# Rounding the next weight block behind the evacuation and the side work, in the stages with transposed results

## The chip, the cores and the metric

The kernel runs on one core of a Trainium2 chip. The metric is the device time of one execution in microseconds; the time before is 1458.11 us, the median of three runs (1457.9 to 1459.06).

## What is computed

Two transformer blocks run on 256 tokens of width 1024, all in float32. The first has an HGRN2 mixer (a gated linear recurrence), a causal multi-scale pooling branch and an MLP with squared ReLU. The second has block attention with a gMLP branch, cross attention over 256 memory rows, and a PEER layer: each token picks 16 of 16384 experts in each of 8 heads by product keys. The core of it is a long row of matrix products, cut to what matters:

```python
proj = x @ w_in                                   # 7 parts of 1024 columns
merged = sigmoid(gate_a) * a + sigmoid(gate_b) * b
x = layer_norm(ALPHA * x + merged @ w_out)
x = layer_norm(ALPHA * x + square(relu(x @ w_up)) @ w_down)
...
y_a = moba_attention(q, k, v) @ moba_w_proj
y_b = gmlp_spatial_gating(gu, gv) @ gmlp_w_proj
x = x + (sigmoid(gate_a) * y_a + sigmoid(gate_b) * y_b) @ w_out
x = x + memory_cross_attention(rmsnorm(x), mem)
x = x + peer_ffn(rmsnorm(x))                      # top-k over product keys
```

The kernel computes the PEER layer over all experts: gelu of the tokens times all down rows, multiplied by a sparse route, times all up rows.

## The kernel before

**Weights.** All weights come as blocks of 128 x 1024 float32 (512 KB), in the fixed order of `plan`: 478 of them. `load` (L122) issues the DMA of one block on SP's queue into a raw buffer (7 of them in the first part of the program, 4 afterwards). `feed` (L138) rounds the block to its high half with one ScalarE copy (L156). `low` (L163) takes the rest, raw minus high, with one VectorE subtraction (L170). TensorE multiplies three times for each 128 x 128 tile: high weights by high input, high by low, low by high (L213 to L215).

**Who decides the order.** The program runs under a manual schedule: TensorE, VectorE and ScalarE execute in the order in which the program writes their instructions. `fill` (L173) feeds blocks until `cap` of them are out (4 in most stages, 5 to 12 around some) and calls `ahead` (L134), which issues the loads for which there is room. `release` (L193) gives a used block back. A new block's rounding has to wait until TensorE has read the block whose buffer it takes.

**Two kinds of stages.** `gemm_n` (L232) gives results with tokens on the partitions, and is not touched. `gemm_t` (L201) gives transposed results, output features on the partitions and 256 tokens as columns. Its outputs come in pairs of 128 features, which share one PSUM bank of `ps_p`; there are two such banks, so a pair can only start when the pair before the last has been evacuated. Where the inner depth is 8 tiles, one weight block is one output of 128 features, and a pair takes two blocks. Where it is 4 (the two projections L1067 and L1077), a block is a whole pair.

**The end of a block** in `gemm_t` (L217 to L225), in this order: release the block, `fill`, evacuate the pair if it is complete (`evac`), then `pump`, `low` and `behind`. `pump` (L93) advances the side work: generators (`hgrn_all` L696, `attend` L915, `gating` L1014, `mem_side` L1049, `routing` L1203, `route` L1334) and closures put off with `later`. `behind` (L321) writes the low halves of results that an evacuation has put off (`split_late` L317).

**Evacuations** that the text speaks of: `evac_sig` (L731, ScalarE tanh, then VectorE); `evac_gate` (L1029: VectorE multiplies by `rall` into `xr` L985, ScalarE tanh L333, VectorE L334); `evac_yb` (L1039, VectorE only, L1040); `evac_a` (L782) and `evac_ya` (L1071): two VectorE operations (L784/785, L1073/1074), then ScalarE rounds the sum (L318), and VectorE takes the low half in `behind` (L323). In the expert stages (`down`, L1321) it is one ScalarE gelu (L1323).

**Side work** that the text speaks of: in `attend` each of four units goes through `scores` (TensorE, VectorE mask L935, ScalarE copies L938), `softmax` (VectorE maximum L900, L901, four ScalarE exponentials L904), a division L909, `turn` (TensorE transposes, ScalarE copies L948) and `output` (ScalarE L329, VectorE L330). `mem_side` runs four ScalarE squares over the memory (L450) and scales it (L1057) by a root that VectorE works out in between. `key_scores` (L1281) copies router scores with ScalarE (L1287) for `routing` on VectorE.

Of the kernel before, what the change touches and what calls it, by code (L numbers as in the profile page):

```python
# [30 lines left out]
def kernel(ctx: ExitStack, tc: tile.TileContext, A: dict, out: bass.AP):  # L31
# [34 lines left out]
    def bp(name, shape=(P, 2, T)):  # L66
        return bank(ps_p, name, shape)
# [4 lines left out]
    def f32(ap):  # L72
        return ap.bitcast(F32)
# [19 lines left out]
    def pump():  # L93
        for s in list(sides):
            s[2] += s[1]
            while s[2] >= 1.0:
                s[2] -= 1.0
                if next(s[0], None) is None:
                    sides.remove(s)
                    break  # L100
        for d in list(deferred):
            d[0] -= 1
            if d[0] <= 0:
                deferred.remove(d)
                d[1]()
# [13 lines left out]
    def room():  # L119
        return 7 if raw_x else 4  # L120
# [13 lines left out]
    def ahead():  # L134
        while plan and plan[0] is not None and len(loaded) + len(half) < room():
            load()

    def feed(beside=None):  # L138

        if not loaded:  # L140
            load()
        raw, kind, cs = loaded.pop(0)
        parts = len(cs)
        wst["out"] += 1
        own, lent = wst["own"] < 4 and kind != 1, 0
        if own:
            wst["own"] += 1
            pc = spl.tile([P, 2, 1024], F32R, tag="w", name="w")
        elif extra:
            pc, lent = extra.pop(0), 1  # L150
        else:
            pc = b8("wb", (P, 2, 1024), F32R)
        for i, x in enumerate(cs):
            if beside:
                beside(i)
            S.activation(pc[:, 0, x], raw[:, x], AF.Copy)  # L156
            if parts > 1:
                V.tensor_tensor(pc[:, 1, x], raw[:, x], f32(pc[:, 0, x]), OP.subtract)
        ready.append((pc[:, 0, :], pc[:, 1, :], own, lent, pc))
        if parts == 1:  # L160
            half.append((pc, raw))

    def low(n=None):  # L163

        if n is None:
            if wst["hold"] or not wst["calm"] and (pend[0] or pend[1]):
                return
            n = 2
        for pc, raw in half[:n]:
            V.tensor_tensor(pc[:, 1, :], raw, f32(pc[:, 0, :]), OP.subtract)  # L170
        del half[:n]

    def fill():  # L173
        while wst["out"] < wst["cap"] and (loaded or plan and plan[0] is not None):
            if (loaded[0][1] if loaded else plan[0][2]) == 2 and wst["own"] >= 4:
                break
            if not loaded and len(half) >= room():
                break
            feed()
        ahead()  # L180

    def take():
        if not ready:
            feed()
        pc = ready.pop(0)
        for i, x in enumerate(half):
            if x[0] is pc[4]:
                low(i + 2)
                break
        low()  # L190
        return pc

    def release(pc):  # L193
        wst["out"] -= 1
        wst["own"] -= pc[2]
        wst["cap"] -= pc[3]
# [4 lines left out]
    def gemm_t(nblk, nk, xs, evac):  # L201

        xh, xl = xs
        pc, f = None, 1024
        for b0 in range(0, nblk, 2):
            ps = bp("pt")
            for j in range(2):
                b, o = b0 + j, ps[:, j, :]
                for k in range(nk):
                    if f == 1024:  # L210
                        pc, f = take(), 0
                    hi, lo = pc[:2]
                    PE.matmul(o, hi[:, f:f + P], xh(b, k, ALL), start=(k == 0), stop=False)  # L213
                    PE.matmul(o, hi[:, f:f + P], xl(b, k, ALL), start=False, stop=False)  # L214
                    PE.matmul(o, lo[:, f:f + P], xh(b, k, ALL), start=False, stop=(k == nk - 1))  # L215
                    f += P
                if f == 1024:  # L217
                    release(pc)
                    fill()
                if j:  # L220
                    evac(b0, 2, ps, ALL)
                if f == 1024:
                    pump()
                    low()
                    behind()  # L225
        behind()
# [94 lines left out]
    def behind():  # L321
        for hi, lo, src in late_lo:
            V.tensor_tensor(lo, src, f32(hi), OP.subtract)  # L323
        late_lo.clear()
# [218 lines left out]
    def proj_fq(u):  # L543
        h0 = u * 4
        fT, kT = h4("fk")
        qT, gc = h4("qg")
        hst[u] = (fT, kT, qT, gc)

        def evac_f(b, n, ps, ts):
            sg = t2("sg", (P, 2, T))  # L550
            S.activation(sg, ps, AF.Tanh, scale=0.5)
            for j in range(2):
                h = h0 + b + j
                V.tensor_scalar(fT[:, b + j, :], sg[:, j, :], oml[:, h:h + 1], lb[:, h:h + 1], op0=OP.mult, op1=OP.add)
            V.tensor_scalar(kT[:, b:b + 2, :], fT[:, b:b + 2, :], -1.0, 1.0, op0=OP.mult, op1=OP.add)

        def evac_q(b, n, ps, ts):
            sg = t2("sg", (P, 2, T))
            S.activation(sg, ps, AF.Tanh, scale=0.5)
            V.scalar_tensor_tensor(qT[:, b:b + 2, :], sg, 1.0, ps, op0=OP.add, op1=OP.mult)  # L560

        gemm_t(4, 8, xk_of(xs), evac_f)
        gemm_t(4, 8, xk_of(xs), evac_q)
# [167 lines left out]
    def evac_sig(dst):  # L731
        def f(b, n, ps, ts):
            sigmoid(dst[:, b:b + n, ts], ps)
        return f

    gemm_t(8, 8, xk_of(xs), evac_sig(sgo))
    gemm_n([evac_v], 8, 1024, xt_of(xs))
    os_, pls = [], []
# [871 lines left out]
```

## Time and profile before

| what | value |
|---|---|
| median of three runs | 1458.11 us |
| the profiled execution's own time | 1457.66 us |
| its span, first to last instruction | 1456.0 us |
| mean granted TensorE clock | 0.998 |
| VectorE busy | 1075.9 us (74%) |
| ScalarE busy | 717.5 us (49%) |
| weight blocks | 478 of 512 KB |

The page gives for each engine the time in which at least one of its instructions ran. TensorE's ends are modelled, so its busy share is not its share at peak. The waits view names, for each idle gap, the instruction that ended it. The windows view counts instructions in a stretch: a matmul over 256 columns comes every 0.112 us at full clock.

### The profile page before, as it was taken

What the parts mean: (1) busy time and instruction counts of PE and PEld (TensorE: products, weight loads), DVE (VectorE), ACT (ScalarE), POOL (GpSimd) and SP (SyncE); (2) the same over time, 40 slices, a digit from 0 to 9 for tenths busy, and PEclk for the clock granted to TensorE, in tenths of its full rate; (3) what the DMA queues carried; (4) which work ended last, traced back from release to release, by engine and by line L of the source; (5) the groups of instructions that cost most, each with busy time, mean ns of one, the idle gap of its engine ahead of it and who ended that gap; (6) DMA issues with size and microseconds to landing.
All of it is one profiled execution on the core that took longest, in us unless ns stands there. A gap on an engine that the chain in (4) does not pass through costs nothing.

```text
span 1456.0 us, 25899 instructions
## 1 busy us (share of the span) xinstructions
PE 1432.4 (98%) x10420; PEld 1304.6 (90%) x10420; DVE 1075.9 (74%) x1895; ACT 717.5 (49%) x933; POOL 33.2 (2%) x68
## 2 busy tenths in 40 slices
PE   8999999999998999999999999999999999999997
PEld 8989998998877899879999999999899787888885
DVE  6867788665498678756999957888645999855555
ACT  5663464554363566644554544444444444444443
POOL 1004000000001000000000000000000000000000
PEclk9999999999999999999999999999999999999999
DMA  8554465566656456515456555455555555555662
GB/s 289 175 160 145 146 222 203 198 215 192 196 181 216 129 191 202 177 55 191 158 174 218 193 190 182 161 174 174 174 189 189 168 180 200 174 190 189 200 191 86
DMA packets 72762, 263.42 MB, mean 181 GB/s; under 512 B 8240, under 2 KB 8752, under 8 KB 72128
## 3 DMA queue, kind: packets, MB, share of 16 engines
q1 hardware_dynamic: 70416, 252.48, 53.7%
q0 software_dynamic: 1936, 8.98, 1.8%
q8 instruction: 82, 1.34, 0.4%
q14 instruction: 40, 0.33, 0.1%
q10 hardware_dynamic: 288, 0.30, 0.1%
HBM read 259.62 MB, written 2.10 MB: 180 GB/s over the span
## 4 chain that ended last, share of the span: by engine, by line
PE 90%; DVE 8%; ACT 1%; issue 1%; DMA 0%; SPq 0%; DVEq 0%; ACTq 0%
PE py L1404 24%; PE pn L247 16%; PE pt L213 15%; PE pt L215 14%; PE pt L214 14%; PE gt L1360 2%; DVE w L170 2%; DVE slots L1194 1%; DVE wb L170 1%; DVE slots L1192 1%; PE hs L637 1%; DVE slots L1197 1%; PE tr L466 0%; PE tr L345 0%; ACT w L156 0%
## 5 line engine op out<-in xcount | busy, mean ns | idle before, releaser
L156 ACT ACTIVATE w<-raw 128x1024 fp32r<-128x1024 f32 (+1 forms) x415 | 435.8, 1051 | 540.1 <-PE pt L215 250.9
L170 DVE TENSOR_TENSOR w<-raw,w 128x1024 fp32r<-128x1024 f32 x409 | 497.8, 1221 | 157.4 <-ACT w L156 156.2
L213 PE MATMUL pt<-h4h,w 128*128 128x256 f32 x1088 | 305.5, 281 | 0.0
L215 PE MATMUL pt<-h4h,w 128*128 128x256 f32 x1088 | 302.4, 278 | 0.1
L214 PE MATMUL pt<-h4l,w 128*128 128x256 f32 x1088 | 302.0, 278 | 0.0
L1404 PE MATMUL py<-w,wh 128*128 128x512 f32 (+1 forms) x1024 | 283.2, 391 | 0.4 <-ACT wh L329 0.4
L1404 PEld LDWEIGHTS py<-w,wh 128*128 128x128 f32 x1024 | 189.4, 188 | 38.9 <-ACT wh L329 0.8
L215 PEld LDWEIGHTS pt<-h4h,w 128*128 128x128 f32 x1088 | 204.9, 188 | 0.8 <-DVE w L170 0.7
L213 PEld LDWEIGHTS pt<-h4h,w 128*128 128x128 f32 x1088 | 204.8, 188 | 0.1
L214 PEld LDWEIGHTS pt<-h4l,w 128*128 128x128 f32 x1088 | 204.6, 188 | 0.1
L1404 PE MATMUL py<-w,wl 128*128 128x512 f32 x512 | 159.4, 390 | 0.2 <-DVE wl L330 0.2
L213 PE MATMUL pt<-xh,w 128*128 128x256 f32 x384 | 110.7, 288 | 5.2 <-ACT w L156 5.2
L1404 PEld LDWEIGHTS py<-w,wl 128*128 128x128 f32 x512 | 96.1, 188 | 20.8 <-DVE wl L330 0.5
L214 PE MATMUL pt<-xl,w 128*128 128x256 f32 x384 | 109.2, 284 | 0.0
L215 PE MATMUL pt<-xh,w 128*128 128x256 f32 x384 | 109.1, 284 | 0.0
L330 DVE TENSOR_TENSOR wl<-slots,wh 128x512 fp32r<-128x512 f32 (+1 forms) x68 | 44.3, 657 | 77.1 <-ACT wh L329 77.1
L213 PEld LDWEIGHTS pt<-xh,w 128*128 128x128 f32 x384 | 74.3, 194 | 5.8 <-ACT w L156 5.5
L170 DVE TENSOR_TENSOR wb<-raw,wb 128x1024 fp32r<-128x1024 f32 x63 | 74.8, 1219 | 5.4 <-ACT wb L156 5.3
L214 PEld LDWEIGHTS pt<-xl,w 128*128 128x128 f32 x384 | 74.0, 193 | 0.4
L215 PEld LDWEIGHTS pt<-xh,w 128*128 128x128 f32 x384 | 73.7, 192 | 0.3
L156 ACT ACTIVATE wb<-raw 128x1024 fp32r<-128x1024 f32 x63 | 63.5, 1048 | 16.0 <-issue 7.4
L1354 DVE TENSOR_TENSOR oo<-oo,rt 128x512 f16<-128x512 f16 x128 | 48.7, 421 | 2.2
(487 smaller groups left out, 2391.0 us busy)
## 6 DMA issues: line engine op xcount, KB each, us to landing
raw<-in_peer_down_dram SPq DMA_DIRECT2D x128, 512.0 KB, 3.5
raw<-in_peer_up_dram SPq DMA_DIRECT2D x128, 512.0 KB, 3.6
raw<-in_w_up_dram SPq DMA_DIRECT2D x32, 512.0 KB, 4.7
raw<-in_w_down_dram SPq DMA_DIRECT2D x32, 512.0 KB, 3.9
raw<-in_w_gb_dram SPq DMA_DIRECT2D x16, 512.0 KB, 3.9
raw<-in_w_ga_dram SPq DMA_DIRECT2D x16, 512.0 KB, 4.6
raw<-in_w_out_dram SPq DMA_DIRECT2D x16, 512.0 KB, 4.0
raw<-in_peer_q_dram SPq DMA_DIRECT2D x16, 512.0 KB, 4.6
```

Source lines behind the costliest of these rows:

```text
L156: S.activation(pc[:, 0, x], raw[:, x], AF.Copy)
L170: V.tensor_tensor(pc[:, 1, :], raw, f32(pc[:, 0, :]), OP.subtract)
L213: PE.matmul(o, hi[:, f:f + P], xh(b, k, ALL), start=(k == 0), stop=False)
L214: PE.matmul(o, hi[:, f:f + P], xl(b, k, ALL), start=False, stop=False)
L215: PE.matmul(o, lo[:, f:f + P], xh(b, k, ALL), start=False, stop=(k == nk - 1))
L247: PE.matmul(o, xx(k, t), ww[:, kk * n + h * 512:kk * n + h * 512 + 512], start=(k == 0 and i == 0), stop=(k == nk - 1 and i == 2))
L330: V.tensor_tensor(lo, src, f32(hi), OP.subtract)
L637: PE.matmul(ps[:, h, :], kk[:, h, tok(t)], qq[:, h, tok(t)], start=True, stop=True)
L1192: V.max(vals[:, c], src)
L1354: V.tensor_tensor(o2[:, i].rearrange("p t (a two) -> p t a two", two=2), q2, turn(1 + i, t0, n), OP.mult)
L1360: PE.matmul(ps[:, u, :], p1[:, u, :], p2[:, i, u, :], start=(i == 1), stop=(i == 2))
L1404: PE.matmul(o, x[:, i % 2, tok(t)], w[:, c], start=(apart[1] == 0 if apart else first and i == 0) and n == 0, stop=(last and i == 7 and n ...
```

## The change

In `gemm_t`, the call of `fill` moves from right behind `release` to behind the evacuation and behind `pump`; `low` and `behind` still follow it. Nothing is added or removed: the same roundings, loads, evacuations and side steps are issued, and the operations of TensorE and VectorE keep their order. On ScalarE the rounding of the next block changes places with the evacuation's and the side work's operations of the same block end; on SP's queue there are only weight loads there, and their order stays.

```diff
@@ -216,11 +216,11 @@
                     f += P
                 if f == 1024:
                     release(pc)
-                    fill()
                 if j:
                     evac(b0, 2, ps, ALL)
                 if f == 1024:
                     pump()
+                    fill()
                     low()
                     behind()
         behind()
```

## Rows read from the trace of the kernel before

**Rows 1.** The page, part 1: busy time and share of the span, by engine.
```profile
PE 1432.4 (98%) x10420; PEld 1304.6 (90%) x10420; DVE 1075.9 (74%) x1895; ACT 717.5 (49%) x933; POOL 33.2 (2%) x68
```

**Rows 2.** Waits of TensorE: total us, times, longest.
```profile
PE rr L980 <- DVE rs_y L426: 3.4, 1, 3.4
...
PE pt L213 <- DVE mg L1073: 0.6, 1, 0.6
...
PE ho L668 <- ACT sx L652: 0.5, 1, 0.5
```

**Rows 3.** Waits of all engines: total us, times, longest.
```profile
DVE w L170 <- ACT w L156: 156.2, 129, 9.3
```

**Rows 4.** Windows: TensorE, weight loads, VectorE, ScalarE, GpSimd busy; clock, DMA, GB/s.
```profile
0.00:20.00 20.00, 14.77 (x85) 13.91 (x86) 11.99 (x30) 12.29 (x19) 4.75 (x27) 1.00 0.90 326
...
300.00:320.00 20.00, 20.00 (x179) 20.00 (x178) 13.58 (x15) 11.71 (x15) 1.05 (x2) 1.00 0.65 192
...
440.00:460.00 20.00, 16.20 (x78) 12.98 (x77) 19.30 (x44) 7.37 (x10) 3.98 (x5) 1.00 0.81 277
...
520.00:540.00 20.00, 20.00 (x177) 19.70 (x177) 14.35 (x21) 12.56 (x23) 0.00 (x0) 1.00 0.50 158
```

**Rows 5.** VectorE's groups from 492 to 574 us: busy, mean ns, idle before.
```profile
L170 DVE TENSOR_TENSOR w<-raw,w 128x1024 fp32r<-128x1024 f32 x20 | 24.4, 1219 | 0.2 <-ACT w L156 0.2
...
L985 DVE TENSOR_TENSOR xr<-pt,rall 128x512 f32<-128x512 f32 x8 | 5.5, 685 | 0.7 <-PE pt L215 0.7
```

**Rows 6.** ScalarE's groups from 492 to 574 us.
```profile
L156 ACT ACTIVATE w<-raw 128x1024 fp32r<-128x1024 f32 x20 | 21.1, 1056 | 11.4 <-PE pt L215 5.6 <-issue 5.5
...
L904 ACT ACTIVATE e<-e,mx 128x256 f32<-128x256 f32 x8 | 4.0, 498 | 3.4 <-DVE mx L901 3.4
...
L1057 ACT ACTIVATE nrm<-mem,rs_y 128x512 f32<-128x512 f32 x4 | 2.7, 716 | 2.6 <-DVE rs_y L426 2.6
L318 ACT ACTIVATE m2h<-mg 128x512 fp32r<-128x512 f32 x4 | 2.5, 630 | 5.6 <-DVE mg L1074 5.6
...
L450 ACT ACTIVATE jk<-mem 128x512 f32<-128x512 f32 x4 | 2.5, 621 | 0.0
```

**Rows 7.** Timeline of ScalarE around a softmax step: start us, us, operation.
```profile
512.12 1.06 ACT L156 ACTIVATE w<-raw 128x1024 fp32r<-128x1024 f32 x1 [0.41 <-PE pt L215]
514.74 0.51 ACT L904 ACTIVATE e<-e,mx 128x256 f32<-128x256 f32 x1 [1.55 <-DVE mx L901]
...
516.72 1.04 ACT L156 ACTIVATE w<-raw 128x1024 fp32r<-128x1024 f32 x1
```

**Rows 8.** Timeline of VectorE in the same stretch.
```profile
514.47 0.17 DVE L901 TENSOR_SCALAR mx<-mx 128x4 f32<-128x4 f32 x1
514.55 1.22 DVE L170 TENSOR_TENSOR w<-raw,w 128x1024 fp32r<-128x1024 f32 x1
515.69 0.68 DVE L985 TENSOR_TENSOR xr<-pt,rall 128x512 f32<-128x512 f32 x1
```

**Rows 9.** Timeline of VectorE in the projection with `evac_ya`.
```profile
564.54 0.69 DVE L1073 TENSOR_TENSOR mg<-pt,sga 128x512 f32<-128x512 f32 x1
...
567.61 0.68 DVE L1073 TENSOR_TENSOR mg<-pt,sga 128x512 f32<-128x512 f32 x1
```

**Rows 10.** Timeline of VectorE at the end of the stage with `evac_a`.
```profile
225.26 0.68 DVE L323 TENSOR_TENSOR ml<-mg,mh 128x512 fp32r<-128x512 f32 x1
```

**Rows 11.** Timeline of ScalarE where the routing starts.
```profile
680.63 1.06 ACT L156 ACTIVATE w<-raw 128x1024 fp32r<-128x1024 f32 x1 [2.14 <-PE pt L215]
681.60 0.58 ACT L1287 ACTIVATE slots<-sk 128x512 f32<-128x512 f32 x1
```

**Rows 12.** Timeline of VectorE there, and waits from 676 to 760 us.
```profile
681.72 1.23 DVE L170 TENSOR_TENSOR w<-raw,w 128x1024 fp32r<-128x1024 f32 x1 [9.27 <-ACT w L156]
...
PEld pt L215 <- DVE w L170: 0.7, 3, 0.3
```

**Rows 13.** The page, part 6: issues, KB each, us from issue to landing.
```profile
raw<-in_w_gb_dram SPq DMA_DIRECT2D x16, 512.0 KB, 3.9
```

## The prediction

> **What bounds the kernel now.** I read the page's busy times first: TensorE runs for 98% of the span [rows 1]. The windows show what that means: 179 matmuls of 256 columns in 20 us, one per 0.112 us, with no gap between them [rows 4]. So a change on ScalarE or VectorE can gain only what TensorE waits for them, and it can lose much more. TensorE's waits that a stage with transposed results can cause are few: 0.6 us for a PSUM bank (`mg` L1073) and 0.5 us for a ScalarE copy (`sx` L652) [rows 2], and 0.7 us for low halves of weights while the routing fills VectorE [rows 12]. That is 1.8 us in all.
>
> The second thing to read is who waits for whom behind TensorE. Over the whole program the low half waits for its rounding for 156 us [rows 3]; VectorE is idle then and nothing is late. But between 492 and 574 us, where the attention runs beside the gates, 20 low halves waited only 0.2 us [rows 5]. There the roundings are ready early: ScalarE issues them as soon as TensorE frees a buffer (5.6 us of waits for L215, [rows 6]) and does the side work after. That is the order which the change turns round.
>
> **The change part by part.** No instruction is added. Three queues see the move. On SP there are only loads, in the same order; a load is issued later only when a low half frees its raw buffer later. A landing takes 3.9 us [rows 13], less than the 8 us that three finished blocks last (24 matmuls of 0.112 us each, [rows 4]), so I cost it at nothing; without that cover it would show as up to 3.9 us per late load. POOL's tiles are not moved. On ScalarE the rounding now starts after the block end's evacuation and side work; on VectorE the low half is still last. A low half starts 1.09 us after its rounding starts (680.63 to 681.72, [rows 11, 12]). So wherever VectorE would have gone straight on to the low half, it now stands still for the step's ScalarE work plus 1.09 us, less what it has to do itself meanwhile. Behind it on VectorE stand the next evacuations, and with only two PSUM banks TensorE waits for these.
>
> *Softmax steps.* Now: rounding at 512.12, maximum done at 514.5, low half at 514.55, then `xr`, which empties a bank, at 515.69 [rows 7, 8]. Afterwards: maximum, first exponential 0.27 us after L901 starts, 1.98 us for four of them (514.74 to 516.72), then the rounding, then 1.09 us. The low half starts 3.34 us after L901 starts and not 0.08: **3.26 us** of standstill. There are two such steps (8 exponentials of this shape, [rows 6]).
>
> *Other steps of that stretch*, by the same rule: the score copies hold the low half up 1.6 us the first time and 0.4 the second, a gate's evacuation (two ScalarE waits on `xr`) 0.3 to 1.1, the four squares over the memory (4 x 0.62) 1.5, the memory's scaling (2 x 0.72 behind a VectorE root) 1.3 and 1.1 [rows 6]. VectorE's present idle time (5.65 us of 20 from 520 to 540, [rows 4]) takes some of it back: I count 0.6 near 520 and 3 near 535 us, the gaps that end by themselves and not with ScalarE.
>
> Adding this from 499 us on, the low half is late by 2.6 us before the first softmax step, 5.8 after it, 6.7 at the second pair of gates, 9.2 after the second softmax step, 9.0 at the end of the gates, and 12 to 13 behind the memory's norm. `xr` now waits for TensorE only 0.7 us in eight [rows 5], and a pair has 5.4 us (48 matmuls) before its bank is needed again. So the first 5 to 6 us of lateness are free, and each further one stops TensorE: 0.75 us at about 528, 2.5 at 544, 2.9 at 551, 2.0 at 564, 3.2 at 570 and 2.4 at 579 us of the new run, each found by laying the late `xr`, `sgb` or `mg` beside the time at which TensorE would be ready.
>
> *The projection with `evac_ya`.* Each block is a pair here, and VectorE's step takes 3.07 us (`mg` to `mg`, [rows 9]). The new cycle is serial: multiply and add 1.44, rounding of the sum 0.54, rounding of the block and low half's start 1.09, low half 1.13, low half of the sum 0.60, together 4.8 us (the operations take 0.68, 0.69, 0.63, 1.06, 1.22 and 0.68, [rows 5, 6, 9], and overlap a little). `mg` at 564.54 moves to 578.3, and TensorE's last block with it: **13.8 us** late, everything in this stretch included. The cycles behind it put the last low half of the sum 2.8 us behind its use in the following product, which needs it 7.4 us after its start (33 matmuls of 512 columns at 0.224 us, twice the 0.112 of [rows 4]); the one before is 0.2 late: **3.0 us**.
>
> *The stage with `evac_a`* has the same cycle, but two blocks to a pair and eight blocks out. Here the last low half of the sum, at 225.26 [rows 10], comes at 231.9; its use comes 7.4 us behind the product's start at 222.6, about 230: **2.0 us**, and 0.2 us for a low half on the way.
>
> *The routing.* VectorE works without a break from 681.7 to 757 us, and at the end TensorE waits for it [rows 12]. Two roundings now stand behind score copies: 681.60 + 0.58 - 0.08 + 1.09 = 683.2 for the first low half (1.5 late, 0.2 of it idle now) and 0.15 more at the fourth. **1.4 us**.
>
> *Gains.* The copy `sx` no longer stands behind a rounding: -0.7 us (0.5 of the wait and its restart). The waits of the expert stages' gelus and of `evac_up` cost nothing: there too three blocks, 8 us, lie ready, and a step is held up 0.6 or 2; without that cover each would cost those.
>
> Sum: 13.8 + 3.0 + 2.2 + 1.4 - 0.7 = 19.7 us, on the profiled execution's 1457.7: 1477.4. The median of the runs shown is 0.4 higher, so 1477.8. **Bounds of the stretch from 492 to 590 us**, which no row shows in the new order: if VectorE took back every standstill up to the projection, there would remain only the projection's own cycles: 1.7 at its bank wait (4.8 less 3.07) and 3.0, 4.7 us. If it took back nothing of the 3.6 us above, 20.4. I take 16.8, since its idle time there is mostly spent waiting for ScalarE, as [rows 5, 6] show, and moves with it.
>
> **The clock.** TensorE stood still once for 3.4 us at about 449 us [rows 2], and the window around it still shows a granted clock of 1.00, 2.4 GHz [rows 4]. The page "TensorE: Matmul & The Clock Gate" of the Trainium skill, section "HAM oscillation", says that gaps between bursts bring the array back to half clock. My waits are no longer than that one, but several lie within 40 us. What a return costs can be read at the start: 85 matmuls where 179 fit, of which the first 5 us held none [rows 4]; (20 - 5) / 0.112 - 85 = 49 missing, about 5 us.
>
> **The rivals.**
> - *Faster:* the earlier evacuation frees banks and copies sooner and the rounding's cover holds. Place and price: the three waits of 1.8 us, so 1456. It decides if the low halves in the attention stretch keep ahead, as three blocks in hand, 8 us, suggest; against it, VectorE is one queue, and lateness passes to `xr` whatever spare the weights have. The page "PSUM — Partial Sum Buffer" of the Trainium skill, section "Summary: rules for kernel authors", speaks for it: it asks to evacuate promptly. By that alone the time would be 1456.
> - *Same:* VectorE's idle time in the attention stretch, 28% from 520 to 540 us [rows 4], takes everything back and the projection's cycles are covered too: 1457 to 1460.
> - *Only the serial cycles cost:* 4.7 + 2.2 + 1.4 - 0.7 = 7.6, with some of the softmax 7.6 to 14: 1465 to 1472, middle 1468.
> - *The clock falls* once or twice in the stretch: 5 to 10 more, 1483 to 1488.
> - That the change does nothing can't be: ScalarE runs in the written order.
>
> **How the numbers follow.** Forecast 0.60 (1472 to 1483, 1477.8 the likeliest), serial cycles alone 0.19, clock 0.08, same 0.08, faster 0.05. The range 1464 to 1486 takes in the first two and half of the third, and leaves out less than 2 in 10. A measurement of this kernel tells 0.2%, some 3 us, from no change. Faster than 1455.2 needs all of its rival and more: 0.03. Within 0.2%: 0.10. Slower: 0.87.
>
> **What would show it.** Right: the low halves (L170) between 492 and 574 us wait some 25 us for L156 in place of 0.2; TensorE waits for `xr` L985, `sgb` L1040 and `mg` L1073, together 10 us or more, and for `m2l` L323 some 3; nearly all the added time lies between 525 and 595 us of the new run, and the last part of the program, from the up projections on, is only shifted. `sx` is gone from TensorE's waits. Wrong: no TensorE wait for L985 (then the standstills are taken back), or lost time that is spread over the expert stages (then a cover that I cost at nothing is gone), or a window below 1.00.

## The result, and the profile after

The changed kernel takes **1476.84 us** (median of 4 runs, 1476.49 to 1478.95) where the kernel before took 1458.01 (4 runs, 1457.83 to 1459.06): a ratio of 1.0134, 95% interval 1.0122 to 1.0147. The forecast was 1477.8. The profiled execution took 1477.13 us with a span of 1475.4.

The page after, part 1 (busy time and share of the span by engine), answers to [rows 1]:

```profile
PE 1440.3 (98%) x10420; PEld 1309.8 (89%) x10420; DVE 1080.0 (73%) x1895; ACT 716.0 (49%) x933; POOL 31.4 (2%) x68
```

The instructions are the same in number. TensorE's busy time is 8 us longer; that is mostly matmuls at a lower clock (mean granted clock 0.993, against 0.998 before; more below). The waits of TensorE after, chosen lines (total us, times, longest), answer to [rows 2]:

```profile
PE pt L213 <- DVE xr L985: 5.6, 3, 2.7
...
PE rr L980 <- DVE rs_y L426: 3.4, 1, 3.4
PE pt L213 <- DVE sgb L1040: 2.4, 1, 2.4
PE pn L247 <- DVE ml L323: 1.9, 1, 1.9
PE pt L213 <- DVE mg L1073: 1.4, 1, 1.4
PE pn L247 <- DVE m2l L323: 1.4, 1, 1.4
```

`xr`, `sgb` and `mg` empty PSUM banks; `ml` and `m2l` are low halves of a sum that the next product reads. All five are VectorE's. Of them only `mg` was among TensorE's waits before; the wait for `rs_y` stood there too, as long as now [rows 2]. `sx` is gone. Who holds VectorE up stands in the waits of all engines after, chosen lines, against [rows 3]:

```profile
DVE w L170 <- ACT w L156: 211.8, 171, 10.6
ACT slots L1323 <- PE pt L215: 110.4, 61, 2.2
```

Over the program the low half waits 56 us longer for its rounding. Most of that costs nothing, as the experiments show. The second line shows the order turned round: in the expert stages it is the evacuation that now stands first in ScalarE's queue and waits for the block. VectorE's groups after, from 492 to 590 us (the stretch is longer now), against [rows 5]:

```profile
L170 DVE TENSOR_TENSOR w<-raw,w 128x1024 fp32r<-128x1024 f32 x19 | 23.3, 1224 | 23.6 <-ACT w L156 23.6
L170 DVE TENSOR_TENSOR wb<-raw,wb 128x1024 fp32r<-128x1024 f32 x7 | 8.5, 1221 | 1.7 <-ACT wb L156 1.7
```

The figure of 0.2 us in [rows 5] is for the blocks in `w` alone; those in the spare buffers (`wb`) waited another 1.0 us in the same stretch before:

```profile
L170 DVE TENSOR_TENSOR wb<-raw,wb 128x1024 fp32r<-128x1024 f32 x7 | 8.5, 1220 | 1.0 <-ACT wb L156 1.0
```

So 1.2 us became 25.3 over the longer stretch, and 20.4 up to 574 us. Here it does cost. One softmax step, first ScalarE's timeline after, then VectorE's (start us, us, operation, idle before), against [rows 7, 8]:

```profile
518.45 0.51 ACT L904 ACTIVATE e<-e,mx 128x256 f32<-128x256 f32 x1 [2.69 <-DVE mx L901]
...
520.44 1.04 ACT L156 ACTIVATE w<-raw 128x1024 fp32r<-128x1024 f32 x1
```

```profile
518.19 0.17 DVE L901 TENSOR_SCALAR mx<-mx 128x4 f32<-128x4 f32 x1
521.51 1.23 DVE L170 TENSOR_TENSOR w<-raw,w 128x1024 fp32r<-128x1024 f32 x1 [3.15 <-ACT w L156]
```

VectorE has finished the maximum and stands still for 3.15 us, because the next thing in its queue asks for a rounding that ScalarE starts only behind four exponentials. From the maximum's start to the low half's it is 3.32 us, where before it was 0.08 [rows 8].

To see where the lateness becomes TensorE's, I laid the start of each matmul in the two traces side by side. TensorE is ahead by 2.6 us at 220 us, behind by 1.2 after the stage with `evac_a`, still by 1.2 at 525 us, by 14.8 at the last block of the projection with `evac_ya`, by 18.0 after the following product, and by 19.0 in the routing, at 757 us of the kernel before. The attention stretch so adds **16.8 us**. Its first bank waits, from TensorE's timeline after:

```profile
529.97 0.36 PE L213 MATMUL pt<-h2h,w 128*128 128x256 f32 x1 [0.52 <-DVE xr L985]
...
545.32 0.36 PE L213 MATMUL pt<-z,w 128*128 128x256 f32 x1 [2.45 <-DVE xr L985]
...
552.15 0.58 PE L213 MATMUL pt<-z,w 128*128 128x256 f32 x1 [2.66 <-DVE xr L985]
```

Nothing for the first 37 us of that stretch, then a wait at bank after bank. Windows, the first line before and the other two after, with the granted clock as the third number from the end:

```profile
540.00:560.00 20.00, 20.00 (x181) 19.39 (x180) 15.55 (x33) 13.70 (x24) 0.00 (x0) 1.00 0.52 159
```

```profile
520.00:540.00 20.00, 19.48 (x174) 18.84 (x174) 12.64 (x18) 9.82 (x20) 0.00 (x0) 1.00 0.43 133
540.00:560.00 20.00, 14.89 (x110) 14.35 (x109) 13.04 (x21) 12.88 (x26) 0.00 (x0) 0.83 0.44 135
```

From 540 to 560 us TensorE started 181 matmuls before and 110 after, and the clock after is below 1.00: behind some of the new waits TensorE multiplied at 1.2 GHz for a few microseconds. That was a rival in the prediction; the account of the prediction below comes back to it.

### The profile page after: what moved, and what is told of

It is laid out like the page before. It is cut to its first block, busy times and chain, and to the rows that moved or that the text cites. A ratio compares the mean times of both kernels' runs of the same rounds, so it can differ in the third digit from the quotient of the medians.

```text
span 1475.4 us, 25818 instructions
## 1 busy us (share of the span) xinstructions
PE 1440.3 (98%) x10420; PEld 1309.8 (89%) x10420; DVE 1080.0 (73%) x1895; ACT 716.0 (49%) x933; POOL 31.4 (2%) x68
## 5 line engine op out<-in xcount | busy, mean ns | idle before, releaser
L156 ACT ACTIVATE w<-raw 128x1024 fp32r<-128x1024 f32 (+1 forms) x415 | 433.2, 1048 | 359.7 <-PE py L1404 181.8
L1323 ACT ACTIVATE slots<-pt 128x512 f32<-128x512 f32 x64 | 38.3, 598 | 110.4 <-PE pt L215 110.4
L156 ACT ACTIVATE wb<-raw 128x1024 fp32r<-128x1024 f32 x63 | 63.4, 1047 | 13.7 <-issue 5.6
```

The lines of the kernel that those rows point to most:

```text
L1323: S.activation(acts(g)[:, 0, b:b + n, :], ps, AF.Gelu_apprx_tanh)
```

## The experiments

In all of them the code is that of the changed kernel but for the edit shown. For the kernels limited to some stages `gemm_t` gets one more argument, so that a call chooses the old or the new place of the rounding:

```diff
                 if f == 1024:
                     release(pc)
+                    late or fill()
                 if j:
                     evac(b0, 2, ps, ALL)
                 if f == 1024:
                     pump()
-                    fill()
+                    late and fill()
                     low()
                     behind()
```

**Where: all but the attention stretch.** `late` everywhere except the two gates and the two projections.

> The old order in the four products beside and behind the attention (both gates, the two projections), the new order everywhere else. The theory (VectorE stands still at the low half, and what is queued behind it empties the PSUM banks late) puts 16.8 us of the change's 18.8 into this stretch: about 1460, with no TensorE wait for xr, sgb or m2l. The rival that lateness of the roundings costs a little in every stage would give back only the stretch's share of the blocks, some 2 us: 1475.

Measured: 1459.34 us beside 1457.73 for the kernel before in the same set, ratio 1.0011 (1.0000 to 1.0022; in brackets the 95% interval, here and below). No wait for `xr`, `sgb` or `m2l`; the one for `ml` is 1.9 us. The rest of the program costs 1.6 us in sum, losses and gains together.

**Where: the attention stretch alone.** `late` in those four calls only.

> The converse: the new order in those four products alone. The theory: 1458 + 16.8 = 1474.8, with the waits for xr, sgb and mg as in the changed kernel. The rival of a cost spread over all stages: 1460. If half of the added time in the stretch were the clock, and the clock fell only because of earlier waits, this run would keep 1.00 there and show some 1469.

Measured: 1473.53 us, ratio 1.0105 (1.0088 to 1.0122). TensorE's waits in it (this kernel has one line more, so L986 is L985 of the others):

```profile
PE pt L213 <- DVE xr L986: 5.6, 3, 2.7
...
PE pt L213 <- DVE sgb L1041: 3.6, 2, 3.0
...
PE pt L213 <- DVE mg L1074: 1.4, 1, 1.4
PE pn L248 <- DVE m2l L324: 1.4, 1, 1.4
```

The four calls bring back the whole set of waits and, laid beside the trace before, 16.8 us between 465 us and the first block after the following product.

**What is passed: evacuation or side work.** The rounding behind the evacuation, but in front of `pump`, everywhere:

```diff
                     evac(b0, 2, ps, ALL)
                 if f == 1024:
-                    pump()
                     fill()
+                    pump()
                     low()
```

> The rounding stands behind the evacuation but in front of the side work, in all these stages. The theory: no softmax, memory or score-copy step holds the low half up any more; the serial cycles of the two stages whose evacuation rounds its own sum stay (4.7 us in the projection, 2 to 4 at the end of the stage with evac_a), so about 1465. The rival that the evacuation in front is what costs: 1475. The rival that only the side work costs: 1458.

Measured: 1463.21 us, ratio 1.0038 (1.0023 to 1.0052). Its waits:

```profile
PE pt L213 <- DVE mg L1073: 2.1, 1, 2.1
...
PE pn L247 <- DVE ml L323: 0.6, 1, 0.6
PE pn L247 <- DVE m2l L323: 0.6, 1, 0.6
PE ho L668 <- ACT sx L652: 0.5, 1, 0.5
```

No `xr`, no `sgb`: without passing the side work they do not come. (An order that passes the side work and not the evacuation was not run.) The serial cycles of the projection stay (`mg`): laid beside the trace before, the stretch adds 4.7 us, 1.5 of them at half clock, which is what the forecast gave these cycles by themselves. And `sx` is back, so its gain too came from passing the side work and not the evacuation.

**Late rounding, or VectorE's standstill?** So far both would do. The next edit puts `low` in front of `fill`:

```diff
                     pump()
-                    fill()
                     low()
+                    fill()
                     behind()
```

> As the change, but the low halves are taken before the new block is rounded, so a low half is always that of an earlier block end and finds its rounding done. The theory: VectorE no longer waits for L156 beside the attention, the waits for xr, sgb and mg go, and what is left is that each low half is one step later on VectorE: up to 3.5 us where the routing leaves no spare, and a little at the first recurrence; about 1462. The rival that the late rounding itself is what TensorE waits for: 1475 or more, as the roundings stand where the change put them.

Measured: 1470.73 us, ratio 1.0088 (1.0072 to 1.0105), and 8 us above what I expected. The waits say why:

```profile
PE pt L213 <- DVE xr L985: 4.0, 3, 2.2
...
PE pt L213 <- DVE sgb L1040: 3.4, 2, 1.9
...
PE pt L213 <- DVE mg L1073: 1.1, 1, 1.1
```

`ml` and `m2l` are gone, the banks are not, and VectorE's low halves in `w` from 492 to 590 us still wait 19.4 us for L156 (23.6 in the changed kernel). The expectation had overlooked a line: `take` (L182), which the next block calls first, runs `low()` too. The low half came back there, still ahead of the next evacuation; all that the edit moved was `behind`, in front of the low half. By itself this tests the serial cycles: 6 us of the 19 go with `ml` and `m2l` and with the half clock that followed `ml` (below).

So `low` in front of `fill` was run once more, and this time `take` no longer issues other blocks' low halves in `gemm_t`:

```diff
-    def take():
+    def take(flush=True):
...
-        low()
+        if flush:
+            low()
         return pc
...
-                        pc, f = take(), 0
+                        pc, f = take(False), 0
```

> The new order of the rounding, and the low half of a block now really one block end later: the call that takes the next block no longer issues it, so at every block end VectorE gets the evacuation and the side work first and then the low half of a rounding that is a whole block (24 matmuls, 2.7 us) old. Theory (VectorE is held up because the low half asks for a rounding that ScalarE has only just been given behind its other work): the low half waits little for its rounding between 492 and 574 us, TensorE's waits for xr, sgb and mg (7.4 us between them in the fully new order, and the lateness behind them) go, as do ml and m2l, and the time falls from 1476.8 us to 1459 to 1463; what stays is routing, where a low half has no spare and comes up to one block later (up to 3.5 us), less the early gains of about 2. Rival (what costs is that the rounding itself starts late, whoever asks for it): TensorE waits for low halves (pt <- w L170) all through the attention stretch and the time stays at 1470 or above.

Measured: 1459.52 us beside 1458.48, ratio 1.0007 (0.9998 to 1.0015). ScalarE's order is that of the changed kernel, with the rounding behind the evacuation and the side work as there, and 17.8 of the 18.8 us are gone. Of VectorE's groups from 492 to 574 us:

```profile
L170 DVE TENSOR_TENSOR w<-raw,w 128x1024 fp32r<-128x1024 f32 x19 | 23.2, 1219 | 0.7 <-ACT w L156 0.7
L170 DVE TENSOR_TENSOR wb<-raw,wb 128x1024 fp32r<-128x1024 f32 x7 | 8.5, 1220 | 0.7 <-ACT wb L156 0.7
```

and behind a softmax's maximum, in VectorE's timeline:

```profile
516.08 0.17 DVE L902 TENSOR_SCALAR mx<-mx 128x4 f32<-128x4 f32 x1
516.16 1.22 DVE L170 TENSOR_TENSOR w<-raw,w 128x1024 fp32r<-128x1024 f32 x1
517.30 0.68 DVE L986 TENSOR_TENSOR xr<-pt,rall 128x512 f32<-128x512 f32 x1
```

The waiting is 1.4 us, as good as the 1.2 before; the low half (of a block rounded earlier) starts 0.08 us behind the maximum's start as in [rows 8], and `xr` follows. No wait for a bank, `ml` or `m2l` is left; what is left is the wait for low halves of weights, 2.6 us: 0.8 in the routing, 0.9 at 147 us, the rest before 200 us, most of it at the start. This settles it: not the late rounding costs, but the VectorE instruction that asks for it at once.

**The early stages alone.** `late` in `evac_f`, `evac_q`, the `sgo` gate, `evac_p` and the `sgb` gate; run in two sets.

> The new order only in the stages before the one with evac_a (evac_f, evac_q, the sgo gate, evac_p, the sgb gate); the old order from there on. Theory: the differences that the two traces show there (TensorE 0.6 us earlier at 45 to 60, 0.6 near 149, 0.8 near 169 us, where the waits for hs and sx stood) are gains of the new order, which nothing gives back later: 1.4 to 2.0 us under the kernel before, 1455.8 to 1456.5 beside 1457.7, and the waits for hs and sx gone. Rival (they are luck of the first loads and are taken back): within 0.3 us of the kernel before, with hs or sx still in TensorE's waits.

> The kernel with the new order only in the stages before the one with evac_a, once more, beside the one above on the same chip. Theory: 1.2 to 1.5 us under the kernel before (0.9987 in the first set), 1 to 1.5 us behind the kernel with each stage's best order. Rival (0.9987 was chance): 0.9995 or above.

Measured: 1456.93 us beside 1458.48, ratio 0.9987 (0.9979 to 0.9996); again 1455.86 beside 1458.33, ratio 0.9981 (0.9972 to 0.9990). A gain, of some 2 us by both medians. The traces show only 0.60 of it at a fixed place: near 149 us the wait for `hs` is gone, in these two and in five others with the new order there. (With the low half a block later it goes too, but 1.1 us are lost right in front of it; with the rounding in front of `pump` 0.1 of it is gained.) The wait for `sx` stayed, against what I expected: it belongs to `evac_b`, which was not among the five (0.78 us near 170 us in each trace where `evac_b` has the new order, but for the one with the rounding in front of `pump`). The 0.6 us near 50 us, which I had read as a third gain, can't be told from scatter: up to 107 us these two executions of one kernel differ by 1.3 us. Where the rest of the medians' 2 us comes from stays open.

**The `sga` gate and the stage with `evac_a` alone**; run in two sets.

> The new order only in the sga gate and the stage with evac_a; the old order elsewhere. Theory: TensorE waits 1.9 us for ml (L324 here) as in the fully new order, 0.3 us on the way, and then multiplies at half clock for some nine matmuls (0.43 us each and not 0.22), 1.8 us more: 1461.5 to 1462.3 beside 1457.7, and a granted clock under 1.00 in the window 226 to 236 us. Rival (the fall of the clock in the fully new order had another cause, earlier in the program): the wait for ml alone, 1459.7 to 1460.2, and 1.00 in that window.

> The kernel with the new order only in the sga gate and the stage with evac_a, once more, for another execution in the profile: the profiled one before kept a granted clock of 1.00 behind its wait of 1.9 us for ml and took 1457.4 us, where the median was 1462.3. Theory (what differs between its executions is whether TensorE's clock falls behind that wait): an execution of 1459 us or more shows half clock between 226 and 240 us (or behind rs_y near 450 to 465 us), one of 1457 to 1458 us shows none. Rival (executions differ by their first loads): no such difference between fast and slow ones.

Measured: 1462.34 us beside 1458.48, ratio 1.0026 (1.0016 to 1.0036); again 1461.32, ratio 1.0022 (1.0012 to 1.0033). Both profiled executions (1457.41 and 1462.0 us) have the wait of 1.9 us for `ml`, 2.5 us of shift with the 0.3 on the way, and a granted clock of 1.00 behind it: the clock term that I expected here did not come. The medians lie 3.9 and 3.0 us above the kernel before, so more than these 2.5; where the rest lies in the executions without a trace stays open. Of the 4.5 us that set the two profiled ones apart, 1.0 was there by 220 us, and 3.4 came at 450 to 460 us; the windows of the first and of the second:

```profile
450.00:460.00 10.00, 7.18 (x35) 5.96 (x35) 9.62 (x22) 1.91 (x3) 1.11 (x1) 1.00 0.76 263
```

```profile
450.00:460.00 10.00, 6.60 (x20) 4.95 (x19) 9.62 (x19) 1.73 (x2) 1.57 (x1) 0.68 0.71 232
```

The kernel is the same, and the wait for `rs_y` in front is nearly so (2.8 and 3.4 us), but there are 35 matmuls in one and 20 in the other: 2.8 us of the 3.4 are the half clock, the rest is the longer wait. The place is one of those that the expectation named.

**The routing alone.** `late` in the stage with `evac_pq` and the gelu groups.

> The new order only in the stages behind the routing's scores (the last projection of queries and the 14 gelu groups); the old order elsewhere. Theory (from 681.7 us on VectorE has no idle time left in which to take back a standstill): TensorE waits longer for the low halves of weights (pt <- w L171 here, 0.7 us before) and ends 1.0 to 1.4 us later, 1458.7 to 1459.1 beside 1457.7; the gelu groups themselves give nothing. Rival (the routing's share of the difference was only a shift by what came before it): within 0.3 us of the kernel before.

Measured: 1460.31 us beside 1458.48, ratio 1.0007 (0.9998 to 1.0016): the median alone decides nothing. The trace does: TensorE loses 0.98 us in two blocks, at 736 and 739 us of the kernel before, and from 730 to 757 us 0.97 to 0.99 in four other traces with this order there, against 0.01 at most in all six with the old. Afterwards 1.3 us more creep in at 0.11 us a block, but the trace of the attention stretch alone has that too, with the old order here, and it is missing in three of the five new ones, so the order does not decide it. Behind the gelu groups come 0.35 us more, here and in the changed kernel.

**The changed kernel once more.**

> The changed kernel itself once more, for another execution in the profile: in the first one TensorE's granted clock fell behind the wait of 1.9 us for ml at 229 us (0.87 and 0.76 in the windows 226:232 and 232:236) and cost 1.8 us, and it stayed at 1.00 behind the wait of 3.4 us for rs_y at 449 us; with the new order in the two stages around ml alone, two executions kept 1.00 behind ml. Theory (each of these waits may or may not be followed by half clock in one execution, and what each fall costs is fixed): the granted clock in 226:236 is 1.00 in this execution or below, and the shift of TensorE against the kernel before is 1.8 us smaller in the first case; the attention stretch adds 16.8 us again, within 0.5, whichever it is. Rival (the fall behind ml belongs to the fully new order): again 0.87 and 0.76, and the same shift.

Measured: 1477.84 us beside 1458.61, ratio 1.0134 (1.0104 to 1.0163); the attention stretch adds 16.7 us. Windows:

```profile
226.00:232.00 6.00, 4.15 (x16) 3.00 (x15) 4.84 (x5) 3.97 (x5) 0.00 (x0) 0.86 0.80 296
232.00:236.00 4.00, 4.00 (x15) 3.21 (x14) 3.43 (x7) 0.42 (x1) 0.00 (x0) 0.79 0.93 312
450.00:460.00 10.00, 6.67 (x18) 5.31 (x19) 9.62 (x21) 1.06 (x1) 1.78 (x1) 0.66 0.70 247
```

The clock fell behind `ml` again, as the rival said (so it did in the kernel with only the attention stretch old), and now behind `rs_y` as well, where the first execution had 1.00. In all three executions that had this wait of 1.9 us and the new order from the start (two of the changed kernel, one of the kernel with the attention stretch old) the clock fell behind it; in the two with the new order only in the `sga` gate and that stage it did not. Why, the runs do not tell.

**Each stage's best order.** `late=1` is the changed order (up to `evac_b`), `late=0` the old one (the `sga` gate, `evac_a`, experts, routing and the rest), `late=2` the low half one block end later (`evac_u`, the gates, both projections; there `take` gets `late < 2` for `flush`, as above). The edit at the end of a block:

```diff
+                    if late == 0:
+                        fill()
                 if j:
                     evac(b0, 2, ps, ALL)
                 if f == 1024:
                     pump()
-                    fill()
+                    if late == 1:
+                        fill()
                     low()
+                    if late == 2:
+                        fill()
                     behind()
```

> Each stage gets the order that did best in it: the new one in the stages up to evac_b (0.6 + 0.6 us there, and 0.8 at the sx copy), the old one in the sga gate, the stage with evac_a, the expert stages and the routing, and in the attention stretch (evac_u, the gates, both projections) the new order with the low half one block end later (0.8 us there, the wait for mg). Theory (the gains are real and add up): 2 to 2.8 us under the kernel before, ratio 0.9981 to 0.9986, and neither hs, sx, mg nor ml in TensorE's waits. Rival (TensorE's wait of 3.4 us for rs_y at 449 us stands behind a chain that does not move, so that it takes back what was gained ahead of it): the gains up to there go into a longer wait for rs_y, and the ratio is 0.9995 or above.

Measured: **1454.72 us** (8 runs, 1453.67 to 1455.97) beside 1458.33, ratio 0.9974 (0.9964 to 0.9985): faster than both kernels. `hs`, `sx`, `mg` and `ml` are gone from TensorE's waits; the wait for `rs_y` is still 3.4 us, so the gains in front of it were not taken back.

## Why the prediction was right, and where two misses met

The forecast fell 1 us from the result, and its mechanism is the one that the runs show. The sum by its steps:

- **Softmax steps**: forecast, a low half 3.34 us after the maximum (L901) starts; measured 3.32.
- **Bank waits in the attention stretch**: forecast 0.75, 2.5, 2.9, 2.0, 3.2 and 2.4 us. From one of these places to the next TensorE's shift, in the second execution of the changed kernel, grows by 0.7, 2.4, 2.8, 2.1, 3.2 and 2.3. In the first execution it grows by 0.7, 2.5, 2.8, 2.7, 2.6 and 2.4. The fourth of these is no wait: TensorE lost it on a block at half clock (552 to 558 us), and found its bank ready behind it. Forecast 13.8, the sums are 13.5 and 13.6, wherever the clock fell: VectorE's chain set the pace, and what half clock took was missing from the next wait.
- **The projection's cycle**: forecast 4.8 us from `mg` to `mg`, against 3.07 in [rows 9]. VectorE's timeline after:

```profile
579.23 0.68 DVE L1073 TENSOR_TENSOR mg<-pt,sga 128x512 f32<-128x512 f32 x1
...
582.28 1.23 DVE L170 TENSOR_TENSOR w<-raw,w 128x1024 fp32r<-128x1024 f32 x1 [1.65 <-ACT w L156]
583.42 0.68 DVE L323 TENSOR_TENSOR m2l<-mg,m2h 128x512 fp32r<-128x512 f32 x1
584.02 0.69 DVE L1073 TENSOR_TENSOR mg<-pt,sga 128x512 f32<-128x512 f32 x1
```

  579.23 to 584.02 is 4.79. The whole stretch: 13.6 up to the projection's last block and 3.2 behind it, in both executions; forecast 13.8 + 3.0. That the second term fits is partly luck: in the first execution 2.1 of the 3.2 come at the low halves of the sum, as forecast, and the rest in the product behind them and the transposes that follow; in the second 1.4 come from half clock and 0.7 at the low halves. The wait for `m2l` is 1.4 and 0.5 us, where some 3 was named.
- **The stage with `evac_a`**: forecast 2.0 for `ml` and 0.2 on the way; measured 2.15 and 0.31 of shift. Here the forecast left a term out: in both executions of the changed kernel TensorE then multiplied at half clock, 1.6 us more. Its timeline in the first:

```profile
229.73 0.50 PE L247 MATMUL pn<-wb,ml 128*128 128x512 f32 x1 [1.85 <-DVE ml L323]
...
230.55 0.63 PE L247 MATMUL pn<-wb,ml 128*128 128x512 f32 x1
...
231.83 0.63 PE L247 MATMUL pn<-wb,ml 128*128 128x512 f32 x1
```

  Three matmuls take 1.28 us, 0.43 each, and not three times the 0.224 us at full clock. The prediction had weighed a falling clock as a rival for the attention stretch, at 5 to 10 us. It fell there too, and cost nothing that can be seen; it cost in the stage where I had not looked for it. The price was read too high as well: about 5 us for a return, from the start of the program, where the falls measured here cost 1.3 to 2.8.
- **The routing**: forecast 1.4 us; measured 1.0. The first low half comes 701.07 - 681.72 = 19.35 us later than in [rows 12], 1.4 more than the 18.0 by which TensorE was then late (forecast 1.5), but only 1.0 of it reaches TensorE.
- **Gains**: forecast 0.7 us for `sx`; measured 0.78 there, and 0.60 at `hs`, which I had not counted: 1.4 us with a place. The medians of the early stages alone give some 2, without `sx`; their rest has no place.
- **Costed at nothing**: the late loads and the expert stages. The loads held, no new wait names one. Of the expert stages 0.35 us were missed, behind the gelu groups.

So 16.8 + 2.5 + 1.0 + 0.35 less the 1.4 with a place is 19.3, and with the 1.6 of the clock 20.9, where the medians differ by 18.8 and the forecast was 19.7. What is between these is less than single executions scatter: 5.5 us among 32 of the kernel before. The agreement within 1 us is partly luck: gains counted too low by 0.7 us or more, the routing too high by 0.4, and a clock term of 1.6 left out.

The signs that the prediction named: the low halves' wait of some 25 us came, as 25.3, but over the lengthened stretch to 590 us. `xr`, `sgb` and `mg` together 9.4 us in the first execution and 10.3 in the second, where 10 was named. A window below 1.00 was named as a sign against it; it came, beside the forecast mechanism and not in its place.

Against the rivals: the two gains with a place, `sx` and `hs`, are steps of the side work. With the rounding behind the evacuation only, `sx` gave nothing and `hs` 0.1 us, so no run shows a gain from an evacuation that is merely issued sooner. The section "Summary: rules for kernel authors" of the page "PSUM — Partial Sum Buffer" in the Trainium skill asks to evacuate promptly. The trace disagrees where VectorE evacuates: issuing the evacuation ahead of the rounding made the next one later, since the low half came to stand still in front of it. With the low half moved as well, the trace agrees: no wait for a bank at all, and 0.8 us gained where `mg` was waited for. The 4.7 us of "only the serial cycles" are what the stretch adds where the rounding stands in front of `pump` and no side work is passed. With the side work passed it is 16.8, the sum in which VectorE's idle time takes back 3.6 us and not everything.

## What to carry to other kernels

When an instruction on one engine is moved back in the order, move back its reader on the in-order queue of the other engine too, by at least as much; else that engine stands still in front of work that had nothing to do with the move. Whether a wait costs is not read from its total (156 us before and 121 in the kernel with the low half a block later were nearly free, some 24 us more in one stretch cost 17) but from what stands behind the waiting instruction and how many buffers that work has. And an order that pays in one stage loses in the next: choose it by stage. Here that gave 1454.72 us, 3.6 under the kernel before.

## What the hardware showed beyond the forecast

Behind one and the same wait TensorE's clock may fall or not. The wait for `rs_y` at 449 us is in all 14 traces of this study, 2.8 or 3.4 us long; behind it the granted clock was below 1.00 in nine and 1.00 in five, the kernel before's among them. The changed kernel had it once each way, and so had the kernel with the new order only at `evac_a`. The fall costs 1.3 to 2.8 us. How much of the scatter between executions it makes is not shown: most of them were not profiled. A wait of 1.9 us for `ml` was followed by half clock three times in five. The section "HAM oscillation" of the Trainium skill's page "TensorE: Matmul & The Clock Gate" says that gaps between bursts bring the array back to half clock; the traces agree that they can, and show that the same gap need not. Two profiles of one kernel can so differ by 2 us or more for a reason that no edit made.
